# Values of an attention projected as rows ahead of it, its running products taken less one, and one copy per output

## The chip, the cores and the metric

The kernel runs on one NeuronCore of a Trainium2 chip. The metric is device time in microseconds (us) of one execution. The core's engines run side by side, each through its own row of instructions in a fixed order: TensorE (PE in the profile; PEld is its weight load) multiplies matrices, VectorE (DVE) and ScalarE (ACT) work element by element, GpSimd (POOL) does some elementwise work and starts transfers, SyncE (SP) starts most transfers. An engine waits at an instruction until what it needs is there, and everything behind it in its row waits too.

## The reference

One decoder layer on 1024 tokens of width 1024: a SwiGLU half layer, a mixer of attention and a state-space model (SSD) side by side, a cross-attention to 256 memory rows, and a second SwiGLU half layer, with RMS norms around each. What the change touches is the mixer's attention with 16 heads of 64 values, on the projections `q`, `k`, `v` of the same normalized tokens:

```python
o_att = stick_breaking_attention(heads(q), heads(k), heads(v))
...
z = jnp.einsum('bhtd,bhsd->bhts', qb, kb) * scale
causal = s_idx[None, :] < t_idx[:, None]
log_1mb = jnp.where(causal, jax.nn.log_sigmoid(-z), 0.0)
suffix = lax.cumsum(log_1mb, axis=3, reverse=True) - log_1mb
a = jnp.exp(jnp.where(causal, jax.nn.log_sigmoid(z) + suffix, -jnp.inf))
outs.append(jnp.einsum('bhts,bhsd->bhtd', a, vb.astype(jnp.float32)))
```

With beta = sigmoid(z), a[t,s] is beta[t,s] times the product of 1 − beta[t,j] over s < j < t. The product c[t,s] of 1 − beta[t,j] over s <= j < t runs backwards along s, and a[t,s] = c[t,s+1] − c[t,s], so the output for token t is a sum of running products c[t,s] times differences of value rows, v[s−1] − v[s], plus the value row v[t] of the token itself.

## The kernel before

**Number format.** Matrix products keep 32 bits by splitting each operand in a high and a low part (`split`, L265: ScalarE casts the high part, VectorE subtracts it from the source for the low one), so one product is three matmuls: high-high, high-low and low-high. `xh`/`xl` are the tokens (features on partitions, two halves of 512 tokens), `whi`/`wlo` a weight tile.

**Staging of the mixer.** The SSD comes first (`ssd`), with the projection of the memory keys woven in at its end (`keys`, evictions on L1491, stores `kv<-Bt`), then the attention (`attention`), then the output projection. Weights come through a stream (`wstream`) that loads one tile ahead, either raw and split on arrival or already split into DRAM earlier (`prepare`, `prepare_all`).

**Attention.** Eight pairs of heads, p = 0 to 7. `inproj(p)` projects `q`, `k` and `v` of the pair, each as two halves (`proj`, 24 matmuls of 512 columns into one of three PSUM banks `mm`), that is 144 matmuls. Queries and keys are evicted, split and sent to other partitions by SyncE (`rows`). For values, a half is evicted with the norm's factor (L1642), the row v[t] is stored to the output array `mix_d` in DRAM (`steps`), the differences `dv` of neighbours are formed on VectorE (L1650 to L1654), transposed on TensorE (`vtr`, four transposes of 128x128 a half) and split into the pair's value tiles V, one for each head.

`units(p)` goes through the two heads (a = 0, 1) and four chunks (c = 0 to 3) of 256 queries. `scores` makes, for each of a chunk's two blocks of 128 queries, one or two score tiles in a PSUM bank `z` (two matmuls each, at most 512 keys wide), the sigmoid of −z on ScalarE (L1746) into `nb`, and the running product on VectorE (a scan, L1750, 128 to 1024 wide), where `begin` (the identity for the diagonal block) restarts the product. Then `values` does the chunk before it: groups of three or four transposes of `nb` into a PSUM bank (`tr`, two banks, and `ms`, one, in turn), a split of each into `ath` (ScalarE, L266) and `atl` (VectorE, L268), and, three groups later (`drain(3)`), four matmuls of 256 columns with V into the chunk's output. `finish` takes the output out of PSUM: ScalarE copies the two halves (products with the high and the low part of V) to 64 partitions (L1763, L1764), VectorE adds them (L1765), and POOL adds the sum to `mix_d` by an accumulating transfer (L1767).

**The order.** TensorE's instructions stand in the order in which the program issues them. For p = 0 to 6 `merge` (L157) advances `units(p)` and `inproj(p + 1)` in turns, in proportion to two planned totals, so that projection matmuls stand between score and value work; pair 7 has other work at its side (`beside`, with the splits of `before`). Rows on the other engines are set by a scheduler after priorities: `urgent` raises that of what it holds. Work put in `later` is issued when a running sum of TensorE's cost passes a given point.

```python
self.run_all(inproj(0))
...
for p in range(7):
    self.merge(units(p), 24000, inproj(p + 1), 32500)
self.merge(tail(), 26000, beside(), 21000 + 5200 * MIXED)
```

## Time and profile before

| | |
|---|---|
| median of 3 runs | 2637.03 us (2636.95 to 2639.56) |
| the profiled execution's own time | 2636.52 us |
| its span, first to last instruction | 2634.7 us |
| mean clock granted to TensorE | 0.994 of full speed |

The profile comes from one execution. A row of a group of instructions names line, engine, operation, the tiles written and read, shapes and count, then the busy time in us, the mean ns of one, and behind the second bar the idle time of the engine just before them with what ended it. A row of the timeline gives start and duration in us, and in brackets the idle time before it. A row of a window gives its bounds and length, then busy us (and instructions) of PE, PEld, DVE, ACT and POOL, the clock granted to TensorE, the share of the transfer engines and GB/s. The durations of matmuls overlap their successors: the pace is read from their starts. A row of transfers gives count, size and the median time from issue to landing. The attention stands between about 1026 and 1590 us of the span; pair p = 2 ends near 1238 us, and a pair's period is about 61 us.

### The profile page before, as it was taken

How to read it: one execution, taken by the hardware profiler on the slowest of the kernel's cores; microseconds unless marked ns; L12 is line 12 of the kernel's file. 1: busy time of each engine (PE TensorE's matmuls, PEld its weight loads, DVE VectorE, ACT ScalarE, POOL GpSimd, SP SyncE). 2: the span in 40 equal slices, each digit the busy share in tenths (PEclk: the TensorE clock that was granted, in tenths of full speed). 3: DMA queues.
4: the chain of work that ended last, by engine and by line, in shares of the span. 5: the costliest groups of instructions: out<-in, count | busy, mean ns of one | idle time of the engine just before them, and what ended most of it. 6: DMA issues, size and time to landing. Idle time of an engine off the chain costs nothing. (4 is left out here: it accounts for less than half of the span.)

```text
span 2634.7 us, 36858 instructions
## 1 busy us (share of the span) xinstructions
PE 2587.8 (98%) x12850; PEld 2155.5 (82%) x12850; DVE 1981.6 (75%) x3044; ACT 1292.3 (49%) x2300; POOL 599.4 (23%) x713
## 2 busy tenths in 40 slices
PE   9899999999999999999999999999999999999999
PEld 7688888778777778888888897888878788888887
DVE  6778887778779775777777777767556888777777
ACT  7434444545356563555555555345544433333553
POOL 2555553110100000111111110101011555452000
PEclk9999999999999999999999999999999999999999
DMA  6558888875655226655555556547558453326554
GB/s 221 170 183 286 278 272 292 279 246 182 240 184 177 81 73 196 173 149 148 141 147 132 170 153 229 192 149 249 197 185 295 140 176 116 100 97 227 188 171 152
DMA packets 212970, 489.82 MB, mean 186 GB/s; under 512 B 26544, under 2 KB 35120, under 8 KB 212784
## 3 DMA queue, kind: packets, MB, share of 16 engines
q1 hardware_dynamic: 163472, 371.58, 42.8%
q0 software_dynamic: 25984, 73.42, 9.2%
q10 hardware_dynamic: 23328, 42.48, 4.3%
q8 instruction: 101, 1.65, 0.3%
q14 instruction: 85, 0.70, 0.1%
HBM read 327.46 MB, written 138.94 MB: 177 GB/s over the span
## 5 line engine op out<-in xcount | busy, mean ns | idle before, releaser
L139 PE MATMUL mm<-xh,whi 128*128 128x512 f32 x1320 | 522.6, 405 | 7.4 <-ACT xh L273 3.0
L139 PE MATMUL mm<-xl,whi 128*128 128x512 f32 (+1 forms) x1252 | 488.1, 390 | 4.7 <-DVE xl L268 4.4
L139 PE MATMUL mm<-xh,wlo 128*128 128x512 f32 x1272 | 489.0, 392 | 0.0
L139 PEld LDWEIGHTS mm<-xh,whi 128*128 128x128 f32 x1320 | 249.1, 189 | 50.3 <-ACT xh L266 3.9
L139 PEld LDWEIGHTS mm<-xh,wlo 128*128 128x128 f32 x1272 | 238.9, 188 | 52.0 <-DVE wlo L268 0.2
L139 PEld LDWEIGHTS mm<-xl,whi 128*128 128x128 f32 x1252 | 236.6, 189 | 39.3 <-DVE xl L268 6.3
L1750 DVE TENSOR_TENSOR_SCAN nb<-nb,begin 128x128 f32<-128x128 f32 (+7 forms) x128 | 171.5, 1352 | 52.4 <-ACT nb L1746 51.9
L1746 ACT ACTIVATE nb<-z,scale 128x128 f32<-128x128 f32 (+2 forms) x192 | 107.7, 580 | 77.8 <-PE z L139 77.5
L268 DVE TENSOR_TENSOR wlo<-wraw,whi 128x1024 fp32r<-128x1024 f32 x70 | 85.4, 1221 | 54.8 <-ACT whi L266 51.4
L266 ACT CAST whi<-wraw 128x1024 fp32r<-128x1024 f32 (+1 forms) x87 | 83.8, 964 | 79.2 <-PE mm L139 55.2
L1767 POOL DMA_DIRECT2D mix<-sq x64 | 52.9, 826 | 229.1 <-DVE sq L1765 131.0
L658 ACT ACTIVATE ft<-ft 128x512 f32<-128x512 f32 x88 | 55.5, 632 | 98.1 <-DVE ft L657 96.1
L139 PE MATMUL dn<-xh,wlo 128*128 128x512 f32 x296 | 101.3, 390 | 0.0
L741 POOL TENSOR_TENSOR wc<-wraw,raw 128x512 f32<-128x512 f32 x56 | 80.3, 1433 | 64.7 <-DVE whi L268 17.8
L741 POOL TENSOR_TENSOR wc<-raw,wraw 128x512 f32<-128x512 f32 x55 | 81.1, 1474 | 51.0 <-DVE blk L268 21.6
L268 DVE TENSOR_TENSOR atl<-tr,ath 128x512 fp32r<-128x512 f32 (+1 forms) x108 | 67.9, 632 | 29.9 <-ACT ath L266 29.5
L826 POOL TENSOR_TENSOR ft<-ft,e 128x512 f32<-128x512 f32 x37 | 59.7, 1613 | 121.1 <-DVE e L825 45.1
L139 PE MATMUL mm<-ath,v 128*128 128x256 f32 x320 | 86.1, 292 | 0.1
L266 ACT CAST ath<-tr 128x512 fp32r<-128x512 f32 (+1 forms) x108 | 58.8, 546 | 55.5 <-PE tr L142 50.9
L139 PE MATMUL dn<-xh,blk 128*128 128x512 f32 x264 | 85.2, 389 | 0.0
L266 ACT CAST wlo<-wc 128x512 fp32r<-128x512 f32 x79 | 49.1, 621 | 71.0 <-PE dn L139 26.1
L139 PE MATMUL mm<-atl,v 128*128 128x256 f32 x320 | 83.1, 282 | 0.7 <-DVE atl L268 0.7
(566 smaller groups left out, 6799.7 us busy)
## 6 DMA issues: line engine op xcount, KB each, us to landing
whi<-dwhi SPq DMA_DIRECT2D x82, 512.0 KB, 3.6
wlo<-dwlo SPq DMA_DIRECT2D x82, 512.0 KB, 4.7
wraw<-in_w_gu SPq DMA_DIRECT2D x43, 512.0 KB, 4.1
raw<-in_w_gu SPq DMA_DIRECT2D x37, 512.0 KB, 4.2
dwhi<-bh SPq DMA_DIRECT2D x66, 256.0 KB, 4.1
dwlo<-bl SPq DMA_DIRECT2D x66, 256.0 KB, 4.3
wraw<-xs SPq DMA_DIRECT2D x56, 256.0 KB, 3.1
xs<-ft ACTq DMA_DIRECT2D x54, 256.0 KB, 3.3
```

What stands on the lines that cost most here:

```text
L139: self._pe(self.nc.tensor.matmul(out, lhsT, rhs, start=start, stop=stop, skip_group_check=self.more), cost)
L266: self.kp(self.nc.scalar.copy(hi, src))
L268: self.nc.vector.tensor_tensor(out=lo, in0=src, in1=hi.bitcast(F32), op=ALU.subtract)
L658: nc.scalar.activation(t, t, AF.Silu)
L741: nc.gpsimd.tensor_tensor(out=t, in0=a, in1=b, op=op)
L826: nc.gpsimd.tensor_tensor(out=t1, in0=t1, in1=e, op=ALU.mult)
L1746: nc.scalar.activation(nb[:, s0:s1], z[:, 0:n], AF.Sigmoid, scale=sc[:, i : i + 1])
L1750: nc.vector.tensor_tensor_scan(out=nb[:, 0:Wd][:, ::-1], data0=nb[:, 0:Wd][:, ::-1], data1=begin[:, S - Wd : S][:, ::-1], initial=0.0, op0 ...
L1767: nc.gpsimd.dma_start(out=self.mix_d[p][a * 64 : a * 64 + 64, csl], in_=o, accum_op=ALU.add)
```

## The change

**Values as rows.** A new `value_rows` projects the values of all 16 heads ahead of `inproj(0)`. Tokens are the stationary operand (128 at a time) and the weights the moving one (512 columns, four head pairs), so that the result has tokens on partitions and needs no transpose. It goes in two halves of the value width, each with four weight tiles (`w_v`, raw, split on arrival), eight blocks of 128 tokens in eight PSUM banks at once (three `mm`, two `z`, two `tr`, one `ms`) and six matmuls for each tile and block: 384 matmuls. ScalarE evicts a block with the norm's factor; POOL's transfers move the block by one row to make v[s−1] (127 rows, and one from the block before); VectorE subtracts; the difference is split and stored to DRAM by POOL, for each of 16 stores as 1024 pieces of 512 bytes. `inproj(p)` fetches the pair's two value tiles (`fetch`, 512 KB each, on SyncE's queue) and projects queries and keys alone: 96 matmuls.

**Running products less one.** `begin` is now a triangle, and evicting the transposes subtracts one: ScalarE by an activation with a bias of −1, VectorE by an operation with a scalar (x − 1 − high part). With c − 1 in place of c the sum needs no value row v[t], so none is stored.

**Output.** `finish` makes one copy of 128x256 on ScalarE, and POOL writes the upper half and accumulates the lower half one output later (`added`). The last output keeps the addition.

**Beside it.** The memory keys' evictions (L1491) are marked urgent. The weight stream of the SSD goes on into the attention, so the value weights are loaded and split at the SSD's end. Sixteen halves of output weights are prepared in the SSD in place of fourteen halves of query, key and value weights there, and none is prepared in the attention. The totals of `merge` are the same as before.

```diff
@@ ssd
-                    nc.vector.tensor_tensor(out=t, in0=ps, in1=rm, op=ALU.mult)
+                    with self.urgent():
+                        nc.vector.tensor_tensor(out=t, in0=ps, in1=rm, op=ALU.mult)
...
-            W = self.wstream(
+            W = self.W = self.wstream(
                 [self.wsrc("ssd", i % 6 if i < 12 else i) for i in range(26)] + [self.wsrc("kv", i) for i in range(8)]
+                + [ap["w_v"][i] for i in range(8)] + [self.wsrc("qk", i) for i in range(16)]
             )
...
-                        [("qkv", i) for i in range(QKV, 24)], *self.prep_pool(wsp),
-                        [self.clock + 9000 + 8000 * i for i in range(2 * (24 - QKV))],
+                        [("out", i) for i in range(8, 16)], *self.prep_pool(wsp),
+                        [self.clock + 9000 + 8000 * i for i in range(16)],
@@ attention
-            self.prepare([("out", i) for i in range(8, 16)], *self.prep_pool(wsp), [self.clock + 30000 + 20000 * i for i in range(16)])
...
-            nc.vector.tensor_copy(begin[:, S - P : S], self.ident)
+            nc.vector.tensor_copy(begin[:, S - P : S], self.tri)
...
-            W = self.wstream([self.wsrc("qkv", i) for i in range(24)])
+            W = self.W
+            V_d = self.value_rows(sp, pp, W)
@@ inproj
-                V = [self.t(sp, [P, 8, P], F32R, "v", bufs=3) for _ in range(2)]
+                V = [self.t(sp, [P, 8, P], F32R, "v", bufs=4) for _ in range(2)]
...
+                def fetch(a):
+                    nc.sync.dma_start(out=V[a].bitcast(F32), in_=V_d[p // 4][:, 2 * (p % 4) + a].bitcast(F32))
...
+                if p:
+                    fetch(0)
                 qevac((yield from self.proj(wq, 0)), h0)
-                qevac((yield from self.proj(wq, 1)), h1)
-                wk = next(W)
-                kevac(evac((yield from self.proj(wk, 0)), 0), h0)
-                wv = next(W)
-                tv = []
-                t0 = evac((yield from self.proj(wv, 0)), 0)
-                tv.append(steps(0, t0, None))
-                v1 = self.proj(wv, 1)
...
+                if p < 7:
+                    qevac((yield from self.proj(wq, 1)), h1)
+                    wk = next(W)
+                    kevac(evac((yield from self.proj(wk, 0)), 0), h0)
+                    if not p:
+                        fetch(0)
+                    fetch(1)
...
                 last = self.proj(wk, 1)
                 for n in range(6):
                     next(last)
                     if p == 7:
                         before(3 + n)
                     yield
-                    if n in (2, 5):
-                        vtr(n // 3, tv[n // 3])
-                        yield
                 kevac(evac((yield from last), 1), h1)
@@ finish
-                    r = slice(64 * n, 64 * n + 64)
-                    tl, o = both[r, 0:256], both[r, 256:512]
-                    nc.scalar.copy(tl, av[64:128, :])
-                    nc.scalar.copy(o, av[0:64, :])
-                    nc.vector.tensor_tensor(out=o, in0=o, in1=tl, op=ALU.add)
-                    csl = slice(c * 256, (c + 1) * 256)
-                    nc.gpsimd.dma_start(out=self.mix_d[p][a * 64 : a * 64 + 64, csl], in_=o, accum_op=ALU.add)
+                    o = both[:, 256 * n : 256 * n + 256]
+                    out = self.mix_d[p][a * 64 : a * 64 + 64, c * 256 : (c + 1) * 256]
...
+                    nc.scalar.copy(o, av)
+                    nc.gpsimd.dma_start(out=out, in_=o[0:64, :])
+                    added()
+                    lows.append((out, o[64:128, :]))
+
+            lows = []
+
+            def added():
+
+                if lows:
+                    out, x = lows.pop()
+                    nc.gpsimd.dma_start(out=out, in_=x, accum_op=ALU.add)
@@ transpose
-                    self.split(ath[:, n0:4, :], atl[:, n0:4, :], tr[:, n0:4, :])
+                    hi, lo, x = ath[:, n0:4, :], atl[:, n0:4, :], tr[:, n0:4, :]
+                    nc.scalar.activation(hi, x, AF.Identity, bias=self.minus)
+                    nc.vector.scalar_tensor_tensor(
+                        out=lo, in0=x, scalar=-1.0, in1=hi.bitcast(F32), op0=ALU.add, op1=ALU.subtract
+                    )
@@ new
+    def value_rows(self, sp, pp, W):
...
+        def shift(tb):
+            x, y = rows[tb]
+            self.kp(nc.gpsimd.dma_start(out=y[1:P], in_=x[0 : P - 1]))
...
+        def differ(n, tb):
+            x, y = rows[tb]
+            self.kp(nc.vector.tensor_tensor(out=y, in0=y, in1=x, op=ALU.subtract))
+            o = rows[n, tb] = self.t(sp, [P, KT, P], F32R, "v", bufs=4)
+            y = y.rearrange("p (h d) -> p h d", h=8)
+            self.split(o[:, :, 0:64], o[:, :, 64:128], y)
+
+        def store(n, tb):
+            self.kp(nc.gpsimd.dma_start(out=V_d[n][:, :, tb].bitcast(F32), in_=rows.pop((n, tb)).bitcast(F32)))
+
+        for n in range(2):
...
+            for q in range(4):
+                wh, wl = next(W)
+                for tb in range(8):
+                    hh, c = tb // 4, slice(tb % 4 * P, tb % 4 * P + P)
+                    for j in range(2):
+                        k = 2 * q + j
+                        b = [w[:, 4 * j : 4 * j + 4, :].rearrange("p a b -> p (a b)") for w in (wh, wl)]
+                        self.mm3(ps[tb], [(self.XH[hh][k][:, c], self.XL[hh][k][:, c], *b)], k == 0, k == 7)
+                    if q < 3:
+                        continue
...
+                    with self.urgent():
+                        nc.scalar.activation(x[:, 0], ps[tb], AF.Copy, scale=self.C[hh][:, tb % 4 : tb % 4 + 1])
+                    at(600, shift, tb)
+                    at(6000, differ, n, tb)
+                    at(8500, store, n, tb)
```

The order of instructions shows where this moves work. Tile numbers stand behind the names; the scan is called SCALAR_TENSOR_TENSOR with `begin` here. On TensorE, at the scores of the second head's third chunk (blocks of 640 and 768 keys) in a middle pair, before:

```order
L139 MATMUL z_12954<-k_12105,q_12103 128x256
L139 MATMUL z_12954<-k_12105,wraw_9838 128x256
L139 MATMUL z_12960<-k_12105,q_12103 128x384
L139 MATMUL z_12960<-k_12105,wraw_9838 128x384
L139 MATMUL mm_12907<-xh_1441_6488,whi_12422 128x512
L139 MATMUL mm_12907<-xl_1493_6699,whi_12422 128x512
L139 MATMUL mm_12907<-xh_1441_6488,wlo_12423 128x512
L139 MATMUL z_12970<-k_12105,q_12103 128x384
L139 MATMUL z_12970<-k_12105,wraw_9838 128x384
L139 MATMUL mm_12907<-xh_1442_6489,whi_12422 128x512
L139 MATMUL mm_12907<-xl_1498_6723,whi_12422 128x512
L139 MATMUL mm_12907<-xh_1442_6489,wlo_12423 128x512
```

The same place now:

```order
L138 MATMUL z_12712<-k_11678,q_11676 128x384
L138 MATMUL z_12712<-k_11678,ql_10397 128x384
L138 MATMUL z_12716<-k_11678,q_11676 128x256
L138 MATMUL z_12716<-k_11678,ql_10397 128x256
L138 MATMUL z_12722<-k_11678,q_11676 128x384
L138 MATMUL z_12722<-k_11678,ql_10397 128x384
L138 MATMUL z_12726<-k_11678,q_11676 128x384
L138 MATMUL z_12726<-k_11678,ql_10397 128x384
L141 MATMUL ms_12731<-ident_112,nb_12685 128x128
L141 MATMUL ms_12731<-ident_112,nb_12691 128x128
L141 MATMUL ms_12731<-ident_112,nb_12685 128x128
L141 MATMUL ms_12731<-ident_112,nb_12691 128x128
```

The triples of projection matmuls (`mm` from `xh`, `xl`) are gone from this place: the four half projections of the next pair end about 20 rows above it, and the next projection matmul comes with the next pair's first scores. On VectorE, from the scan of 384 keys of the second head to its scan of 896 or 1024, before:

```order
L1750 SCALAR_TENSOR_TENSOR nb_12911<-nb_12911,begin_9832 128x384
L1750 SCALAR_TENSOR_TENSOR nb_12920<-nb_12920,begin_9832 128x512
L268 TENSOR_TENSOR atl_12928<-tr_12926,ath_12927 128x384
L1750 SCALAR_TENSOR_TENSOR nb_12946<-nb_12946,begin_9832 128x640
L1750 SCALAR_TENSOR_TENSOR nb_12959<-nb_12959,begin_9832 128x768
L216 TENSOR_TENSOR bl_12967<-braw_12505,bh_12966 128x512
L268 TENSOR_TENSOR atl_12981<-tr_12979,ath_12980 128x512
L268 TENSOR_TENSOR xl_2199_9847<-mm_12907,xl_2198_9846 128x512
L268 TENSOR_TENSOR atl_12999<-ms_12997,ath_12998 128x384
L1765 TENSOR_TENSOR sq_2191_9831<-sq_2191_9831 64x256
L1750 SCALAR_TENSOR_TENSOR nb_13036<-nb_13036,begin_9832 128x896
L1750 SCALAR_TENSOR_TENSOR nb_13049<-nb_13049,begin_9832 128x1024
```

And now:

```order
L1733 SCALAR_TENSOR_TENSOR nb_12685<-nb_12685,begin_9823 128x384
L1733 SCALAR_TENSOR_TENSOR nb_12691<-nb_12691,begin_9823 128x512
L1787 SCALAR_TENSOR_TENSOR atl_12699<-tr_12697,ath_12698 128x384
L1733 SCALAR_TENSOR_TENSOR nb_12711<-nb_12711,begin_9823 128x640
L1733 SCALAR_TENSOR_TENSOR nb_12721<-nb_12721,begin_9823 128x768
L1787 SCALAR_TENSOR_TENSOR atl_12733<-ms_12731,ath_12732 128x512
L1787 SCALAR_TENSOR_TENSOR atl_12746<-tr_12744,ath_12745 128x384
L1733 SCALAR_TENSOR_TENSOR nb_12761<-nb_12761,begin_9823 128x896
L1733 SCALAR_TENSOR_TENSOR nb_12771<-nb_12771,begin_9823 128x1024
L1787 SCALAR_TENSOR_TENSOR atl_12783<-tr_12781,ath_12782 128x512
L1787 SCALAR_TENSOR_TENSOR atl_12800<-ms_12798,ath_12799 128x512
```

The prepared weights (`bl`), the projection's split (`xl`) and the output's addition (`sq`) are gone from between the scans; scans and evictions of transposes follow one another. On VectorE around the last memory keys, ahead of the attention, before:

```order
L268 TENSOR_TENSOR Bt_9682<-sq_2160_9716,Bt_9682 128x256
L1491 TENSOR_TENSOR sq_2165_9752<-mm_9727,Ct_9206 128x256
L268 TENSOR_TENSOR dg_9890<-mm_9862,sq_2212_9889 128x512
L268 TENSOR_TENSOR Bt_9754<-sq_2165_9752,Bt_9754 128x256
L1491 TENSOR_TENSOR sq_2168_9782<-mm_9757,Ct_9206 128x256
```

And now:

```order
L267 TENSOR_TENSOR wlo_9896<-wraw_9893,whi_9895 128x1024
L267 TENSOR_TENSOR Bt_9683<-sq_2160_9717,Bt_9683 128x256
L1491 TENSOR_TENSOR sq_2165_9753<-mm_9728,Ct_9207 128x256
L339 RECIPROCAL cy_2172_9794<-cy_2172_9794 128x8
L267 TENSOR_TENSOR Bt_9755<-sq_2165_9753,Bt_9755 128x256
L1491 TENSOR_TENSOR sq_2171_9789<-mm_9764,Ct_9207 128x256
```

A split of value weights (`wlo` from `wraw`) has come in ahead of the last keys, and the first split of query rows (`dg`) is gone from between them; the last key's eviction still stands behind the split `Bt` of the key before it.

76 lines of the change are left out of this document (44 added, 32 removed).

## Prediction

> **What bounds the kernel now.** First the page's busy shares, then its matmul rate in windows of one head pair each.
>
> ```profile
> span 2634.7 us, 36858 instructions
> PE 2587.8 (98%) x12850; PEld 2155.5 (82%) x12850; DVE 1981.6 (75%) x3044; ACT 1292.3 (49%) x2300; POOL 599.4 (23%) x713
> ```
>
> ```profile
> 1177.20:1238.30 61.10, 60.45 (x355) 52.43 (x354) 45.11 (x64) 34.20 (x72) 9.21 (x24) 1.00 0.55 151
> ```
>
> TensorE is busy 98% of the span, and in a head pair's period of 61.1 us for all but 0.65 us (61.10 − 60.45), at full clock. VectorE is busy 45.11 of the 61.1 us there, so a saving in TensorE's work saves time as long as VectorE keeps up. Where it doesn't already, the groups of TensorE's instructions between 1060 and 1483 us (the end of pair 0 and pairs 1 to 6) tell, the waits standing last; the timeline shows one such wait.
>
> ```profile
> L142 PE MATMUL tr<-ident,nb 128*128 128x128 f32 x329 | 50.8, 273 | 2.2 <-DVE atl L268 1.4 <-DVE v L268 0.8
> L142 PE MATMUL ms<-ident,nb 128*128 128x128 f32 x160 | 24.9, 273 | 1.7 <-DVE v L268 1.6
> L142 PE MATMUL tr<-ident,dv 128*128 128x128 f32 x36 | 5.4, 272 | 0.0
> L142 PE MATMUL ms<-ident,dv 128*128 128x128 f32 x20 | 3.0, 272 | 0.0
> ```
>
> ```profile
> 1175.29 0.28 PE L139 MATMUL mm<-atl,v 128*128 128x256 f32 x1
> 1176.36 0.52 PE L142 MATMUL ms<-ident,nb 128*128 128x128 f32 x3 [0.80 <-DVE v L268]
> ```
>
> TensorE's only waits are at the pair ends, for VectorE's evictions of transposes: 2.2 + 1.7 = 3.9 us over six pair ends. Counted in starts, the one shown is 1176.36 − 1175.29 less 0.12 for the matmul itself, 0.95 us against the profile's 0.80; with 0.15 more each, all six are 4.8.
>
> **The change part by part.** It is costed by TensorE's pace, from starts in the timeline near the end of a pair:
>
> ```profile
> 1169.10 0.34 PE L139 MATMUL z<-k,q 128*128 128x384 f32 x1
> ...
> 1169.44 0.39 PE L139 MATMUL mm<-xh,whi 128*128 128x512 f32 x1
> ...
> 1170.14 0.39 PE L139 MATMUL z<-k,q 128*128 128x512 f32 x1
> ...
> 1170.60 0.40 PE L139 MATMUL mm<-xh,whi 128*128 128x512 f32 x1
> ...
> 1171.76 0.60 PE L142 MATMUL ms<-ident,dv 128*128 128x128 f32 x4
> 1172.19 0.60 PE L142 MATMUL tr<-ident,nb 128*128 128x128 f32 x4
> ```
>
> A score pair takes 0.34 us at 384 columns and 0.46 at 512; four transposes 0.43; a 512-column matmul half of 0.46, 0.23, and a 256-column one 0.12.
>
> *Values moved.* 8 pairs x 48 matmuls become one block of 384 ahead of inproj(0), 384 x 0.23 = 88 us at either place: 0.
>
> *Transposes of the value differences.* 64 of them go, in 16 groups of 0.43: **−7.0**. (The rows above show 56, those in that stretch.)
>
> *Old waits at pair ends.* Their releasers, the splits of transposed values (L268, v), go, or their place moves: five of the six are gone, 4.8 x 5/6: **−4.0**; the sixth, before pair 7, belongs to the p = 6 term.
>
> *The fill.* The merge still advances scores and values by 24000 against 32500 for the projections, but inproj(p + 1) is now 4 half projections (96 matmuls) and not 6 (144). By the order, it is used up before the scores of the second head's second chunk. From there to the end of the pair TensorE has scores, transposes and products alone, where before a triple of projection matmuls stood between nearly all of them. VectorE's work for that stretch is unchanged in kind: it is now a chain against less TensorE work. Its durations, and ScalarE's last:
>
> ```profile
> L268 DVE TENSOR_TENSOR atl<-tr,ath 128x512 fp32r<-128x512 f32 x31 | 21.2, 684 | 12.3 <-ACT ath L266 12.1
> L1750 DVE TENSOR_TENSOR_SCAN nb<-nb,begin 128x1024 f32<-128x1024 f32 x8 | 18.2, 2276 | 1.2 <-ACT nb L1746 1.2
> L1750 DVE TENSOR_TENSOR_SCAN nb<-nb,begin 128x896 f32<-128x896 f32 x8 | 16.2, 2024 | 6.2 <-ACT nb L1746 6.2
> L1750 DVE TENSOR_TENSOR_SCAN nb<-nb,begin 128x768 f32<-128x768 f32 x8 | 14.0, 1753 | 0.1
> L1765 DVE TENSOR_TENSOR sq<-sq 64x256 f32<-64x256 f32 x32 | 13.4, 419 | 6.1 <-ACT sq L1764 5.5
> L268 DVE TENSOR_TENSOR atl<-tr,ath 128x384 fp32r<-128x384 f32 x23 | 12.6, 546 | 1.3 <-ACT ath L266 1.3
> L1750 DVE TENSOR_TENSOR_SCAN nb<-nb,begin 128x640 f32<-128x640 f32 x8 | 11.9, 1492 | 12.0 <-ACT nb L1746 12.0
> ...
> L1750 DVE TENSOR_TENSOR_SCAN nb<-nb,begin 128x512 f32<-128x512 f32 x8 | 9.8, 1225 | 2.5 <-ACT nb L1746 2.5
> L1750 DVE TENSOR_TENSOR_SCAN nb<-nb,begin 128x384 f32<-128x384 f32 x8 | 7.7, 958 | 7.2 <-ACT nb L1746 7.2
> ```
>
> ```profile
> L1746 ACT ACTIVATE nb<-z,scale 128x384 f32<-128x384 f32 x40 | 23.2, 579 | 26.0 <-PE z L139 26.0
> ```
>
> ```profile
> L275 DVE SCALAR_TENSOR_TENSOR xl<-S,params,xh 128x512 fp32r<-128x512 f32 x16 | 11.2, 746 | 1.2 <-ACT xh L273 1.2
> ```
>
> Scans 384 to 1024: 0.96 + 1.23 + 1.49 + 1.75 + 2.02 + 2.28 = 9.73. The eviction of four transposes is now x − 1 less the high half, a form with a scalar, as L275: 0.75 for 0.68, and by the same step 0.61 for 0.55. Between the first of these scans and the transposes that wait, the order has four: 0.61 + 0.75 + 0.61 + 0.75 = 2.72. Neighbours on VectorE overlap by about 0.08 (an estimate), 9 x 0.08 = 0.7 off. Ahead of the first scan lie its score pair and sigmoid, 0.34 + 0.58, and some 0.2 of handing on. The chain: 9.73 + 2.72 − 0.7 + 1.1 = 12.8 us.
>
> TensorE's work over the same stretch: five score pairs of 384, four of 512, one of 256 and the next pair's 128 and 256: 1.70 + 1.84 + 0.24 x 2 + 0.17 = 4.2; three groups of four transposes and three of three, 3 x 0.43 + 3 x 0.33 = 2.3; six products of 4 x 0.12, 2.9; two triples of projections, 1.4. Sum 10.8. The wait is 12.8 − 10.8 = 2.0 us, mostly in front of the next pair's first transposes, whose bank is freed behind the scan of 1024. For p = 0 to 5: 6 x 2.0 = **+12.0**. It can't be under zero; if VectorE is still at work on earlier rows when the stretch begins (the last projection's eviction and split, 2 x 0.68), it is 2.8 each. Bounds 0 and +17.
>
> At the end of p = 6, VectorE's order has more ahead of the scan of 1024: four splits of 0.75 for pair 7's side work, the last key's eviction and split of 0.68 each, and two evictions of transposes that stand behind that scan in other pairs (0.75 + 0.61). 12.8 + 3.0 + 1.4 + 1.4 − 0.6 (overlaps) = 18.0, so the wait is 18.0 − 10.8 = 7.2 at most; some of the splits may run in idle time. I take **+6**, bounds +2 and +8.
>
> *The block's start.* All eight banks are taken at once; its third block waits for the bank of the last memory key (L1491). VectorE and the stores there before:
>
> ```profile
> 1027.78 0.42 DVE L1491 TENSOR_TENSOR sq<-mm,Ct 128x256 f32<-128x256 f32 x1
> 1032.86 0.69 DVE L268 TENSOR_TENSOR dg<-mm,sq 128x512 fp32r<-128x512 f32 x1 [4.66 <-ACT sq L266]
> ```
>
> ```profile
> kv<-Bt SPq DMA_DIRECT2D x3, 512.0 KB, 4.0
> ```
>
> The last key's eviction stands behind a split that waits for a store of 4.0 us to land, about 1027.7 + 4.0 = 1031.7, while the block reaches its third bank near 1029: +2.7. Marking the evictions urgent moves one of them by a sum (0.7), at a wait of TensorE near 1015: −0.7. **+2**, bounds −0.7 and +3.5. The three splits of value weights that join VectorE's row there (1.22 us each) stand in front of evictions that are awaited only at that same bank.
>
> *The output.* One copy of 128x256 for two of 64x256, no VectorE addition (8 x 0.42 us a pair off VectorE), and two transfers for one on POOL's queue. The addition isn't in the chain above: 0. The copy after next waits for a transfer to land:
>
> ```profile
> mix<-sq POOLq DMA_DIRECT2D x53, 64.0 KB, 2.9
> ```
>
> Write and accumulation one after the other are 2 x 2.9 = 5.8 us, in which ScalarE may stand, at two outputs that come soon after each other; VectorE's lag of 2 us covers part. 0, bound +1.5 a pair. Preparation of 16 halves of output weights moves out of attention into the part before it, in place of 14 others, on engines that TensorE doesn't wait for there: 0.
>
> *The clock.* What a wait of 2 us does to TensorE's granted clock:
>
> ```profile
> 1017.47 0.36 PE L139 MATMUL mm<-xs,whi 128*128 128x256 f32 x1 [1.93 <-DVE sq L1491]
> ```
>
> ```profile
> 1018.50:1021.80 3.30, 3.30 (x18) 3.30 (x17) 0.18 (x1) 0.41 (x1) 0.00 (x0) 0.50 0.65 262
> 487.30:490.70 3.40, 3.17 (x13) 2.28 (x14) 3.40 (x7) 2.71 (x6) 0.00 (x0) 1.00 0.65 214
> ```
>
> ```profile
> 487.27 0.96 PE L139 MATMUL dn<-hl,dx 128*128 128x512 f32 x3 [2.74 <-ACT F L1064]
> ```
>
> A wait of 1.93 us was followed by half clock, one of 2.74 by full clock, so the length alone doesn't decide; 3.4 us at half clock cost 1.7 us. Of the seven new waits of 2 us and more I let three cost that, since the rows go one to one: **+5**, bounds 0 and +12. [...]
>
> **The sum.** −7.0 − 4.0 + 12.0 + 6 + 2 + 5 = +14. The profiled execution took 2636.5 us (span 2634.7 and 1.8 around it), half a us under the median of 2637.03. 2636.5 + 14 = 2650.5, against the median 2651.
>
> **The rivals.**
> - *VectorE isn't late.* It loses 8 x 0.42 us of additions, the value evictions, differences and splits in each pair, so it may start the stretch with scans in hand. If the wait per pair falls under 0.5 us, the clock holds, and the end of pair 6 costs 2: −7 − 4 + 3 + 2 + 0 = −6, 2631. Deciding point: 1.0 us a pair, where gain and cost balance at about 2637 to 2639. For it speaks 45 busy of 61 us; against it, that this is a mean, and the scans of the second head stand last in the pair in the row of VectorE. 0.12; within 0.2% (under 5.3 us, about what a measurement can tell from no change), at 1 us each, 0.14.
> - *The value rows come late.* Each of 16 stores cuts its 512 KB into 1024 pieces of 512 bytes on POOL's queue, and the differences on VectorE stand in front of the queries' evictions of inproj(0).
>
> ```profile
> q0 software_dynamic: 25984, 73.42, 9.2%
> ```
>
>   A packet there takes 0.092 x 16 x 2634.7 / 25984 = 0.15 us of one engine, larger ones than these; 64 to an engine are up to 9.6 us a store, 77 for eight, while the half block after them lasts 44. If the second half's shifts queue behind them, VectorE stands for some 20 us with three banks of 24 matmuls, 5.5 us each, as cover: +5 to +15 on top, 2656 to 2666. 0.16. [...]
> - *Every wait halves the clock, and ScalarE's wait for the accumulation adds 1 us a pair.* 7 x 1.7 = 12 for 5, and +7: 2665. 0.10.
>
> **How the numbers follow.** The forecast, 2643 to 2658: 0.48. Late rows 0.16, clock and ScalarE 0.10: slower 0.74 in all. Same 0.14, faster 0.12. The range goes from 2636, which leaves out the rival on the other side and a little of "same", to 2666, which leaves out the late rows' upper end.
>
> **What would show it.** The period of a pair falls from 61.1 to about 52 us (61.1 less 48 x 0.23, less 0.9 of transposes, less 0.8 of waits, plus 2 and some clock). The groups of TensorE's transposes show waits of 10 us and more for VectorE's evictions or scans in pairs 0 to 5, in place of 3.9, and none for value splits; granted clock of 0.50 stands behind some. The value block lasts 88 us with a wait of 2 to 3 near its start. Wrong would be: waits under 0.5 us at pair ends (the first rival), waits of the projections in inproj(0) for VectorE (the second), or waits for ScalarE's copies.

## The result, and the profile after

The changed kernel takes 2663.6 us (median of 4 runs, 2661.2 to 2665.7) against 2637.0 for the kernel before on the same chip: a ratio of 1.0099, 95% interval 1.0082 to 1.0117, slower by 26.6 us in the medians. The profiled executions differ by 24.7 us (span 2659.4 for 2634.7), and all sums below are made against that.

The page of the changed kernel and, from the windows, one middle pair of heads (p = 3):

```profile
span 2659.4 us, 36677 instructions
PE 2589.6 (97%) x12786; PEld 2148.0 (81%) x12786; DVE 1939.3 (73%) x2925; ACT 1287.7 (48%) x2229; POOL 661.7 (25%) x819
```

```profile
1297.04:1347.42 50.38, 49.18 (x298) 42.39 (x297) 36.23 (x43) 29.59 (x56) 13.87 (x33) 1.00 0.53 136
```

TensorE isn't busy for less: the time has gone into its waits. What it waited for between 980 and 1640 us (us in total, times, the longest; of the lines, L138 holds the matmuls, L141 the transposes, L1729 the sigmoid, L1733 the scan, L1786 and L1787 the evictions of transposes, L1491 that of the memory keys):

```profile
PE z L138 <- DMA k<-dg: 12.7, 1, 12.7
PE z L138 <- ACT nb L1729: 8.7, 14, 2.3
PE mm L138 <- DVE sq L1491: 5.5, 2, 4.3
PE tr L141 <- DVE nb L1733: 2.5, 2, 2.3
PE ms L138 <- DVE atl L1787: 1.7, 1, 1.7
```

The longest row is one wait: the first scores of pair 0 wait for transfers of key rows (`k<-dg`, their low parts). In the timeline of TensorE, three of its four largest waits there (the fourth, of 2.28 us, is shown with pair 6 below):

```profile
1028.78 0.50 PE L138 MATMUL mm<-whi,xh 128*128 128x512 f32 x1 [4.28 <-DVE sq L1491]
...
1149.48 0.44 PE L138 MATMUL z<-k,q 128*128 128x128 f32 x1 [12.68 <-DMA k<-dg]
...
1508.81 0.55 PE L141 MATMUL tr<-ident,nb 128*128 128x128 f32 x3 [2.32 <-DVE nb L1733]
```

Cut at the same instructions, read from their starts in both traces:

| stretch | before | after | difference |
|---|---|---|---|
| up to the last norm of the SSD (`ms<-small,yacc`) | 1024.8 | 1019.6 | −5.2 |
| from there to pair 0's first scores | 35.4 | 129.9 | +94.4 |
| pair 0 | 55.9 | 47.5 | −8.4 |
| pairs 1 to 5 | 305.4 | 251.2 | −54.2 |
| pair 6 | 61.7 | 56.2 | −5.4 |
| pair 7 and up to the last norm (`ms<-small,asum`) | 117.7 | 123.0 | +5.3 |
| the rest | 1033.9 | 1032.0 | −1.9 |

The moved projections are 48 matmuls a pair, 11.0 us at 0.2285 from one start to the next. Seven pairs' worth moves up: 76.8 us out of the third to fifth row into the second. What is left is +17.6 before pair 0, +2.6 in pair 0, +0.6 in pairs 1 to 5 together, +5.6 in pair 6, +5.3 in pair 7, and −7.1 outside. Of the 5.2 us gained ahead, 2.9 are there already near 770 us, where the instructions of both kernels are the same: windows at half clock lie elsewhere in the two executions, before at 550.9 to 557.7 and 670.3 to 673.8 us, now at 486.8 to 493.7.

Half clock behind the two longest waits, and while TensorE stood, in windows of the changed kernel:

```profile
1029.60:1032.90 3.30, 3.30 (x9) 2.65 (x8) 0.03 (x1) 0.00 (x0) 0.41 (x1) 0.50 0.39 159
1139.00:1149.40 10.40, 0.00 (x0) 0.00 (x0) 0.93 (x2) 1.90 (x2) 0.00 (x0) 0.50 0.92 250
1149.50:1155.80 6.30, 6.30 (x17) 5.14 (x18) 2.07 (x3) 1.42 (x3) 0.00 (x0) 0.50 1.04 291
```

The first and the third cost 1.7 and 3.2 us of work at half speed; the second cost nothing, since TensorE waited. So the 17.6 and 2.6 us around pair 0's start are 12.7 + 3.2 for the key rows, and 4.3 + 1.7 for the last memory key's bank, 21.9 in all, less 1.7 for the four groups of transposes of value differences (0.43 each) that are gone from these two stretches.

**Why the key rows came late.** ScalarE in that place, then the transfers issued from 1100 to 1150 us (count, size, median us to landing):

```profile
1135.18 0.62 ACT L265 CAST sq<-ev 128x512 fp32r<-128x512 f32 x1 [2.93 <-DMA q<-sq]
1144.53 0.62 ACT L265 CAST xl<-ev 128x512 fp32r<-128x512 f32 x1 [8.73 <-DMA q<-xl]
```

```profile
v<-v POOLq DMA_DIRECT2D x8, 512.0 KB, 8.3
...
q<-sq SPq DMA_DIRECT2D x4, 128.0 KB, 7.7
q<-xl SPq DMA_DIRECT2D x4, 128.0 KB, 7.6
```

The split of the first key half waits until the first query half's rows have left the same buffer, the second likewise. Those rows take 7.7 us to land, where they took 4.9 in the kernel before at the same place and 3.5 in its pair 2. Eight stores of value rows, 512 KB each, are under way; that these are the reason is tested below (e5). SyncE's own issue of them stretches too:

```profile
1131.96 3.07 SPq L1631 DMA_DIRECT2D q<-xl  x2
1135.12 1.87 SPq L1631 DMA_DIRECT2D wraw<-xl  x1
```

so that the key rows, behind them in SyncE's row, are issued at 1142.8 us only. The first key half is split by 1138.6 already, and SyncE's row has no gap of more than 0.3 us from 1121.1 to 1142.8: what ended last is that row, not the buffer. TensorE had finished all 96 projections at 1136.8.

### The profile page after: what moved, and what is told of

The parts are those of the page before. It is cut to its first block, busy times and chain, and to the rows that moved or that the text cites. A ratio compares the mean times of both kernels' runs of the same rounds, so it can differ in the third digit from the quotient of the medians.

```text
span 2659.4 us, 36677 instructions
## 1 busy us (share of the span) xinstructions
PE 2589.6 (97%) x12786; PEld 2148.0 (81%) x12786; DVE 1939.3 (73%) x2925; ACT 1287.7 (48%) x2229; POOL 661.7 (25%) x819
## 4 chain that ended last, share of the span: by engine, by line
PE 82%; DVE 7%; issue 4%; DMA 4%; ACT 2%; POOL 1%; SPq 0%; DVEq 0%; ACTq 0%; POOLq 0%
PE mm L138 42%; PE dn L138 31%; PE z L138 2%; DVE nb L1733 2%; PE ms L138 1%; PE tr L141 1%; PE y L138 1%; PE ms L141 1%; PE seg L138 1%; PE tr L138 1%; DVE atl L1787 1%; PE st L138 0%; DVE hl L267 0%; SPq L1631 0%; DMA oraw<-mix 0%
## 5 line engine op out<-in xcount | busy, mean ns | idle before, releaser
L138 PE MATMUL mm<-xh,whi 128*128 128x512 f32 x1192 | 470.0, 404 | 3.6 <-ACT xh L265 2.7
L138 PE MATMUL mm<-xl,whi 128*128 128x512 f32 (+1 forms) x1124 | 438.6, 390 | 4.7 <-DVE xl L267 4.1
L138 PE MATMUL mm<-xh,wlo 128*128 128x512 f32 x1144 | 439.0, 392 | 0.0
L138 PEld LDWEIGHTS mm<-xh,whi 128*128 128x128 f32 x1192 | 225.3, 189 | 45.5 <-ACT xh L265 3.9
L138 PEld LDWEIGHTS mm<-xh,wlo 128*128 128x128 f32 x1144 | 215.2, 188 | 46.6 <-DVE wlo L267 0.4
L138 PEld LDWEIGHTS mm<-xl,whi 128*128 128x128 f32 x1124 | 212.6, 189 | 39.1 <-DVE xl L267 6.2
L1733 DVE TENSOR_TENSOR_SCAN nb<-nb,begin 128x128 f32<-128x128 f32 (+7 forms) x128 | 169.9, 1349 | 57.0 <-ACT nb L1729 56.8
L267 DVE TENSOR_TENSOR wlo<-wraw,whi 128x1024 fp32r<-128x1024 f32 x78 | 95.3, 1222 | 89.1 <-ACT whi L265 88.7
L1729 ACT ACTIVATE nb<-z,scale 128x128 f32<-128x128 f32 (+2 forms) x192 | 105.4, 582 | 68.4 <-PE z L138 68.0
L138 PE MATMUL dn<-xh,wlo 128*128 128x512 f32 x296 | 101.2, 390 | 0.0
L1786 ACT ACTIVATE ath<-tr,small 128x512 fp32r<-128x512 f32 (+1 forms) x106 | 68.3, 646 | 50.9 <-PE tr L141 49.1
L1787 DVE SCALAR_TENSOR_TENSOR atl<-tr,ath 128x512 fp32r<-128x512 f32 (+1 forms) x106 | 65.7, 625 | 36.0 <-ACT ath L1786 35.5
L138 PE MATMUL z<-k,q 128*128 128x128 f32 (+2 forms) x192 | 68.0, 358 | 21.4 <-DMA k<-dg 12.7
L138 PE MATMUL mm<-ath,v 128*128 128x256 f32 x320 | 88.6, 299 | 0.0
L138 PE MATMUL dn<-xh,blk 128*128 128x512 f32 x264 | 85.2, 389 | 0.0
L138 PE MATMUL mm<-atl,v 128*128 128x256 f32 x320 | 83.2, 282 | 0.5 <-DVE atl L1787 0.5
```

The source lines that it names most:

```text
L138: self._pe(self.nc.tensor.matmul(out, lhsT, rhs, start=start, stop=stop, skip_group_check=self.more), cost)
L267: self.nc.vector.tensor_tensor(out=lo, in0=src, in1=hi.bitcast(F32), op=ALU.subtract)
L1729: nc.scalar.activation(nb[:, s0:s1], z[:, 0:n], AF.Sigmoid, scale=sc[:, i : i + 1])
L1733: nc.vector.tensor_tensor_scan(out=nb[:, 0:Wd][:, ::-1], data0=nb[:, 0:Wd][:, ::-1], data1=begin[:, S - Wd : S][:, ::-1], initial=0.0, op0 ...
L1786: nc.scalar.activation(hi, x, AF.Identity, bias=self.minus)
L1787: nc.vector.scalar_tensor_tensor(out=lo, in0=x, scalar=-1.0, in1=hi.bitcast(F32), op0=ALU.add, op1=ALU.subtract)
```

## The experiments

The runs were made at different times, each beside runs of the kernel before (medians of 2636.99 to 2639.61), so the ratio to it, or the difference of the two medians, is what compares. Of the first three experiments the intervals overlap with the changed kernel's; what they did is read from their traces. Each edit is made to the changed kernel. One more, e5, leaves out work, was executed once, and has no interval.

| run | ratio to the kernel before | interval | us above the kernel before |
|---|---|---|---|
| the change | 1.0099 | 1.0082 to 1.0117 | 26.6 |
| e1_k_second | 1.0085 | 1.0069 to 1.0100 | 24.4 |
| e2_whole_rows | 1.0076 | 1.0061 to 1.0091 | 21.2 |
| e3_mm_banks_last | 1.0069 | 1.0054 to 1.0084 | 20.1 |
| e4_fill_even | 1.0044 | 1.0028 to 1.0061 | 12.3 |
| e6_two_copies | 1.0108 | 1.0091 to 1.0126 | 29.8 |
| e7_values_after_pair0 | 1.0066 | 1.0051 to 1.0081 | 18.4 |
| e8_first_even_banks | 1.0032 | 1.0019 to 1.0045 | 8.5 |
| e9_three_together | 1.0019 | 1.0007 to 1.0030 | 5.5 |
| e10_and_fetch_late | 1.0022 | 1.0012 to 1.0032 | 5.6 |
| e11_cover_for_pair0 | 1.0010 | 1.0001 to 1.0018 | 2.9 |
| e12_cover_and_block_later | 1.0028 | 1.0018 to 1.0038 | 8.0 |

### The key rows of pair 0

**e1: keys in the second place.**

```diff
-                    qevac((yield from self.proj(wq, 1)), h1)
+                    if p:
+                        qevac((yield from self.proj(wq, 1)), h1)
                     wk = next(W)
                     kevac(evac((yield from self.proj(wk, 0)), 0), h0)
                     if not p:
+                        qevac((yield from self.proj(wq, 1)), h1)
                         fetch(0)
```

> Pair 0 alone projects in the order q, k, q, k of the halves (it was q, q, k, k), so that the first half of the keys is evicted 24 matmuls (5.5 us) earlier, into the split buffer that no transfer holds; the two fetches stand behind the second query half. Theory A (the first keys wait for the split buffer that the first queries' transfers still hold, and have only 24 matmuls as cover): the wait of 12.7 us at pair 0's first scores falls to about 4, and half of the 17 us at half clock goes, 2663.6 - 8.7 - 1.5 = about 2653. Theory B (all transfers there are slow because the value stores fill the engines, whatever the order): the wait stays above 9, 2660 or more.

Median 2663.3. TensorE's waits:

```profile
PE z L138 <- DMA k<-xl: 4.8, 1, 4.8
PE z L138 <- issue: 2.7, 1, 2.7
```

The one wait of 12.7 us has become two, 2.7 at the first scores (for which the profile names no releaser) and 4.8 when the second half of the keys is needed. From the SSD's end to pair 1 the trace is 3.7 us shorter, less than half of what theory A gave. The order was one cause, but the run can't tell how: the edit gives the keys another buffer and also moves their rows ahead of the second query half's in SyncE's row. The slow landing stays, now on the other half.

**e2: the value rows stored whole.**

```diff
-        V_d = [self.tc.dram_tile([P, 8, KT, P], F32R, name=self.nm("v")) for _ in range(2)]
+        V_d = [self.tc.dram_tile([P, KT, 8, P], F32R, name=self.nm("v")) for _ in range(2)]
...
-out=V_d[n][:, :, tb].bitcast(F32)
+out=V_d[n][:, tb].bitcast(F32)
```

> The value rows lie in DRAM as they are stored: a store is 128 pieces of 4 KB in place of 1024 of 512 bytes, and a pair's fetch takes the small pieces in its place. Theory B: the stores land in about 4 us in place of 7.0, the query and key rows in 3 in place of 7.7, and the wait of 12.7 us falls under 5, about 2653. Theory A alone: the stores aren't what the rows wait for, the wait stays at 10 or more, 2660 to 2665. If the fetch in small pieces holds up SP's queue in every pair, waits for k or v come in at pair starts and it is slower than 2664.

Median 2660.0. The stores landed in 6.0 us where it was 7.0, and the wait was 11.0 us for 12.7. In e6, which doesn't touch this, it was 11.0 as well, so the pieces' size did next to nothing: theory B, as it put it by pieces, falls. The bytes are the same. The median, by the table 5.4 us better than the change, does not speak for the pieces either: the intervals overlap, and the traced execution took 2664.2 us.

**e5: no stores of the second half.**

```diff
-                    at(8500, store, n, tb)
+                    if not n:
+                        at(8500, store, n, tb)
```

> Leaves out the eight stores of the second half's value rows (pairs 4 to 7 then fetch those of pairs 0 to 3, so heads 8 to 15 get other heads' values); all else as changed. In the changed kernel the transfer engines were 97 to 99% busy from 1113 to 1137 us, with 4 MB of these stores, and finer or coarser pieces made no difference. Theory (the bytes of the stores make the query and key rows land in 7.7 us): without them the rows land in 4 us or less and the wait of 12.7 us at pair 0's first scores falls to 3 or less with no half clock, about 2648. Rival (SyncE's slow issue, 1.2 to 1.9 us for one row transfer there, has another reason, or the split buffers alone): the wait stays above 7.

One execution, 2651.0 us. The transfers from 1100 to 1150 us, and TensorE's wait:

```profile
q<-sq SPq DMA_DIRECT2D x5, 128.0 KB, 2.9
...
k<-dg SPq DMA_DIRECT2D x2, 128.0 KB, 3.1
```

```profile
PE z L138 <- DMA k<-dg: 0.3, 1, 0.3
```

The wait is gone with the half clock behind it. As far as one execution tells, that is 12.1 us above the kernel before (2638.95 beside it) where the change is 26.6. The stores are what the key rows waited for, by their bytes rather than their pieces (e2): from 1113 to 1137 us the transfer engines are busy 0.94 of the time in the changed kernel's trace (not the 97 to 99% of the expectation) and 0.86 here, and one row's issue on SyncE takes 0.5 to 1.0 us again. With the rows landing in 2.9 us the buffers no longer hold anything up either, so e1's cause is a consequence of this one.

### The last key's bank, and the fill

**e3: the mm banks last.** In the list of eight banks `z`, `z`, `tr`, `tr`, `ms` come first and the three `mm` behind them.

> The block's eight banks are taken in another order: z, z, tr, tr, ms first and the three mm banks, which the memory keys still hold, for the last three token blocks. If the 4.3 us near 1025 are the wait for the last key's eviction, they go, with the 3.4 us at half clock behind them: 2663.6 - 4.3 - 1.7 = about 2657.5. Rival: the block then waits at its eviction end or the queries' first half waits for an mm bank, and nothing is gained: 2663.

Median 2659.0, by the table 6.5 us less than the change, about the 6.0 expected. The wait of 4.3 us is gone and with it the window at half clock near 1030; of the row for L1491 the wait near 1015 is left:

```profile
PE mm L138 <- DVE sq L1491: 1.3, 1, 1.3
```

**e4: the fill spread over the pair.**

```diff
-                self.merge(units(p), 24000, inproj(p + 1), 32500)
+                self.merge(units(p), 24000, inproj(p + 1), 20700)
```

> The merge gets 20700 in place of 32500 for the four half projections, so that they last to the end of each pair. Where the fill ran out, the trace of the changed kernel shows waits of scores for sigmoids (1.5 us a pair in starts, pairs 1 to 5), and 2.3 + 0.4 + 0.7 + 2.3 us at the end of pair 6. Theory (the fill's end makes them): they go in pairs 0 to 5 (6 x 1.5 = 9 us) and 3 of pair 6's 5.7, about 2652. Rival (VectorE's and ScalarE's work is what the pair now takes): the waits spread over the pair and the period stays at 50.4 us, 2660 or more.

Median 2651.2, by the table 14.3 us less than the change, the most of any single edit that leaves no work out. A middle pair, and the waits for sigmoids that are left (8.7 in the changed kernel):

```profile
1345.00:1393.91 48.91, 48.64 (x298) 42.40 (x297) 36.31 (x43) 30.07 (x57) 13.86 (x32) 1.00 0.58 141
```

```profile
PE z L138 <- ACT nb L1729: 4.0, 8, 1.3
```

The pair takes 48.9 us for 50.4, with the same 36 us of VectorE, so the fill's end, not the pair's work, made the waits. In the traces pairs 0 to 5 are 8.0 us shorter, against the 9 expected. Pair 6 and what follows up to the last norm are 5.6 shorter: the waits for scans are gone there, those of scores for sigmoids are down to 1.3 and 1.1, and no half clock follows.

### The output

**e6: two copies and the addition, as before the change.**

```diff
-                    nc.scalar.copy(o, av)
-                    nc.gpsimd.dma_start(out=out, in_=o[0:64, :])
+                    nc.scalar.copy(tl, av[64:128, :])
+                    nc.scalar.copy(o, av[0:64, :])
+                    nc.vector.tensor_tensor(out=o, in0=o, in1=tl, op=ALU.add)
+                    nc.gpsimd.dma_start(out=out, in_=o)
...
```

> Undoes the output part alone: two copies of 64x256 on ScalarE, VectorE's addition, one plain transfer of POOL for each output, no accumulation. VectorE gets 8 x 0.42 us a pair, ScalarE 8 x 0.37. If the output part gave anything it is in the stretch without fill, where two outputs fall: scores wait longer by up to 0.37 an output there, +3 to +5 over seven pairs, 2667 to 2669. Rival (the wait for the accumulation to land costs ScalarE as much): 2663, no difference.

Median 2668.7, by the table 3.2 us worse than the change, though the intervals overlap. In the trace the period of pair 3 is longer by 0.6 us, as the expectation had it:

```profile
1294.97:1345.95 50.98, 49.37 (x298) 42.39 (x297) 39.23 (x51) 32.81 (x65) 7.05 (x24) 1.00 0.46 124
```

With the change, ScalarE's copies wait for the accumulation to land (10.5 us over pairs 1 to 5, six times). In those pairs TensorE has no more than a wait of 0.3 us near them, for an eviction, and e6, without accumulation, has the same one. In pair 6 it is otherwise (below).

### Other orders, and the edits together

**e7: the value block behind pair 0's queries and keys.** `run_all(inproj(0))` stands ahead of `value_rows`, pair 0's fetches behind it; the raw tiles and three of the token blocks use other buffers.

> The queries and keys of pair 0 are projected first, the value block behind them (its raw tiles and blocks in other buffers; the weight stream in that order), and pair 0's fetches behind the block. The rows of queries and keys then have 88 us to land, and the last memory key's bank isn't awaited, since the projections take banks one at a time. Theory: 12.7 us and their 3.3 of half clock go, and 4.3 with 1.7 of half clock; pair 0's scans now share VectorE and ScalarE with the second half's differences and splits (16 of 0.69 on VectorE), which costs 2 to 6 in pair 0. 2663.6 - 22 + 4 = about 2646. Rival (the second half's value rows then hold up pair 0 by as much): 2655 or more.

Median 2657.4, against the 2646 expected. The waits for key rows and for the last key's bank are gone, as expected, but pair 0 takes 56.5 us for 47.5: its scores and transposes wait for ScalarE and VectorE, in whose rows the second half's differences and splits now stand. The rival comes nearer.

**e8: e7, e3 and e4 together.**

> The order of the values behind pair 0's queries and keys, the mm banks last in the block, and the fill spread over each pair (20700). The savings add if they are at different places: 2646 - 12 = about 2634, level with the kernel before or a little under. Rival (the even fill takes from pair 0 what the order gave): 2640 or more.

Median 2647.5, the rival's side, not the 2634 of the expectation. Pair 0 and pair 1 in windows:

```profile
1133.75:1195.02 61.27, 49.24 (x255) 40.78 (x253) 40.10 (x49) 31.50 (x57) 19.58 (x37) 0.92 0.69 203
1195.02:1243.93 48.91, 48.65 (x297) 42.42 (x296) 35.41 (x41) 29.53 (x55) 12.60 (x30) 1.00 0.55 139
```

In pair 0 TensorE has 42 matmuls fewer than in pair 1 (fewer transposes and products, which follow one chunk behind the scores) and takes 12.4 us longer all the same: it waits 12.0 us, and three windows of 3.4 us are at half clock.

**e9: e1, e3 and e4 together.**

> The fill spread (20700), the mm banks last, and pair 0's halves in the order q, k, q, k, together, with the value block ahead of pair 0 as changed. If the three savings lie at three places they add: 2663.6 - 12.4 - 4.6 - 3.7 (the last from the traces, from the SSD's end to pair 1) = about 2643. The first scores still wait for k rows, 3 to 5 us twice. Rival: the even fill gives pair 0 more to do while the second half's stores run, 2648.

Median 2644.1: by the table 21.1 us less than the change, where the three alone give 2.2 + 6.5 + 14.3 = 23.0, so within the intervals (some 3 us each way) the savings add. Two waits are left where the key rows are needed, 4.5 us (no releaser named) and 5.0.

**e10: e9 with pair 0's fetches behind its keys.**

> As the run before, and pair 0's two fetches (1 MB) stand behind the second half of its keys on SyncE's queue instead of ahead of it. If the second wait (4.8 us for k rows, with half clock) is made by the 1 MB ahead of them, it goes: 2643 - 5 = about 2638. Rival: the values come late instead, pair 0's first products wait by 2 to 5 us, and the sum is level with the run before.

Median 2644.1. The expected 5 us didn't come: the second wait isn't shorter but longer, 7.4 us. The megabyte of the fetches wasn't what it waited for.

**e11: e9, with 17 triples of pair 1's projections ahead of pair 0's scores.**

```diff
-                self.merge(units(p), 24000, inproj(p + 1), 32500)
+                fill = inproj(p + 1)
+                for _ in range(0 if p else 17):
+                    next(fill)
+                self.merge(units(p), 24000, fill, 20700 if p else 9700)
```

> The three edits together (fill spread, mm banks last, pair 0 in the order q, k, q, k), and 17 of the 32 triples of projections for pair 1 stand ahead of pair 0's first scores (11.7 us), the other 15 being spread over pair 0. If the waits for pair 0's key rows (4.5 and 5.0 us, and 6.8 us of half clock after them) are a lack of other work for TensorE while the transfers are held up by the value stores, they go, and pair 0 with half its fill pays about 2 us: 2644.1 - 9.5 - 3 + 2 = about 2633.5, faster than the kernel before by 0.2%. Rival (pair 0 with half the fill is bound by VectorE and ScalarE): 2640 or more.

Median 2642.5, ratio 1.0010, the nearest to the kernel before, but in the rival's range and not the 2633.5 expected. The wait of TensorE is now one place further, in the projections themselves:

```profile
PE mm L138 <- DVE xl L267: 6.5, 1, 6.5
```

The third `mm` bank is held by a half whose split waits for a buffer that rows under way still hold (ScalarE's longest wait for `k<-xl` is 6.5 us there). Cover by more projections fills banks, not time.

**e12: e8 with the same 17 triples.**

> The same 17 triples ahead of pair 0's scores, with the value block behind pair 0's queries and keys. Here pair 0 waited for sigmoids and evictions (1.85 + 2.3 + 1.4 + 2.9 + 3.1 us, and three windows at half clock) while the second half's differences and splits ran on VectorE and ScalarE; the 11.7 us cover most of that: 2647.5 - 9 = about 2638. Rival: VectorE's row keeps the same work and pair 0 ends no sooner, 2645.

Median 2647.6, as e8: the rival's time. The trace has another reason for it than VectorE's row. ScalarE stands in front of splits of value differences whose buffer a store (`v<-v`) still holds, and TensorE's two longest waits, for sigmoids, end right behind. ScalarE, then TensorE:

```profile
1147.77 0.62 ACT L268 CAST v<-nb 128x512 fp32r<-128x512 f32 x1 [7.23 <-DMA v<-v]
...
1156.86 0.62 ACT L268 CAST v<-nb 128x512 fp32r<-128x512 f32 x1 [3.52 <-DMA v<-v]
```

```profile
1150.61 0.44 PE L138 MATMUL z<-k,q 128*128 128x384 f32 x1 [3.42 <-ACT nb L1733]
...
1158.01 0.69 PE L138 MATMUL z<-k,q 128*128 128x384 f32 x1 [3.12 <-ACT nb L1733]
```

So behind pair 0's projections, too, it is the stores that the block's new place runs into, here by the buffers that they hold. No run takes these waits away alone.

No version is faster than the kernel before. Not tried: a store of half the bytes (the differences before their split), and a second half of the value block spread over later pairs.

## Why the prediction was right, and where it wasn't

The direction was right, and the time lies in the range (2636 to 2666), near its upper end. The forecast of 2651, +14, was half of the +26.6 measured and the time lies outside the likeliest case's own range of 2643 to 2658. That the range holds it is in part luck: the largest cost was in no term of the sum. By its steps:

- **Values moved, "0".** This is the step that failed. TensorE's work is the same at either place, but the step moved two other things: 48 matmuls of cover went from between pair 0's first keys and its scores, and 4 MB of stores came in ahead of the rows that these scores need. That cost 12.7 us and 3.2 of half clock. e5 takes both away by the stores alone, with no cover added. The rival of late value rows had the stores and the right time (2656 to 2666, given 0.16), but another path: VectorE would have been held up by the differences. VectorE did stand 21.2 us in front of a difference, but in the value block, where nothing waited for it. ScalarE did stand in front of a difference's split, ahead of that of the second query half, until a store let go of the buffer:

```profile
1129.07 0.62 ACT L265 CAST v<-k 128x512 fp32r<-128x512 f32 x1 [3.00 <-DMA v<-v]
```

  But SyncE was then still at the first query half's rows, up to 1130.5 us, and began the second's at 1132.0, so this is worth 1.5 us of the 12.7 at most; what was late were SyncE's rows.
- **Transposes, −7.0, and old waits, −4.0.** TensorE has 12786 matmuls for 12850, the 64 transposes less, 0.86 us a pair, and none of its waits is for a split of values any more: right.
- **The fill, +12.0.** The size is right: pairs 1 to 5 took 61.08 us each, 48.3 without the moved matmuls (10.97), the transposes (0.86) and the old wait (0.95), and take 50.24 now, so some 1.9 a pair for 2.0 forecast. The place in the order is right too, as e4 shows. The path is wrong, by the sign that the prediction itself set: the waits at the pair ends, for VectorE's evictions, are 0.32 to 0.34 us, under its 0.5. Most of the cost, 1.5 us in starts, is ahead of them: the scores wait for a `z` bank, which ScalarE's sigmoid frees (0.44 and 0.43 us as idle time, the two in each pair). Pair 3's end and the start of the next:

```profile
1339.80 0.44 PE L138 MATMUL z<-k,q 128*128 128x384 f32 x1 [0.44 <-ACT nb L1729]
...
1343.74 0.50 PE L138 MATMUL z<-k,q 128*128 128x512 f32 x1 [0.43 <-ACT nb L1729]
...
1349.74 0.66 PE L141 MATMUL tr<-ident,nb 128*128 128x128 f32 x4 [0.32 <-DVE atl L1787]
```

  The overlap of neighbours on VectorE that the chain took off, 0.08 us, is what the trace of before shows (a split of 0.68 us from 1167.88 us on, the next from 1168.48). The chain was priced too dear by its evictions: a group of four is 0.68 us by the form with a scalar, where 0.75 was taken,

```profile
L1787 DVE SCALAR_TENSOR_TENSOR atl<-tr,ath 128x512 fp32r<-128x512 f32 x40 | 27.0, 680 | 18.1 <-ACT ath L1786 18.1
L1786 ACT ACTIVATE ath<-tr,small 128x512 fp32r<-128x512 f32 x40 | 27.7, 694 | 23.4 <-PE tr L141 23.3 <-issue 0.2
```

  and the dearer part of x − 1 is ScalarE's, 0.69 us for the 0.59 of the plain cast. It had not been costed at all, and it is ScalarE that TensorE then waits for; no run takes this part away alone, so its share is not shown.
- **The end of pair 6, +6.** Pair 6 lost 5.6 us beside the moved matmuls; 1.7 of them are half clock, counted below, and 0.9 of transposes saved stand against them, so its waits are 4.8. The last 2.3 of its chain fall into pair 7: 7.1, inside the bounds of 2 to 8. Only these 2.3 are on the path that was forecast, a transpose waiting for VectorE's scan. The longest of the others, 2.28 us, is a wait for a sigmoid, and ScalarE in front of it stood at the side work for pair 7 and then at a copy, each time for a transfer, the second the accumulation:

```profile
1488.46 0.72 ACT L272 ACTIVATE xh<-ev,params 128x512 fp32r<-128x512 f32 x1 [1.45 <-DMA ev<-mix]
1490.87 0.37 ACT L1755 COPY sq<-mm 128x256 f32<-128x256 f32 x1 [1.69 <-DMA mix<-sq]
```

```profile
1492.86 0.44 PE L138 MATMUL z<-k,q 128*128 128x384 f32 x1 [2.28 <-ACT nb L1729]
```

  Without the accumulation (e6) that wait is still 1.67 us, with ScalarE 1.99 us in front of `ev<-mix`, so the accumulation is the smaller part.
- **The block's start, +2.** 4.3 us for the bank of the last key against 2.7 forecast, and 1.26 near 1015 for the 1.93 before (0.7 less, as forecast): 3.6. e3 confirms the cause. The half clock behind it was not in this term.
- **The output, 0.** e6 makes it a gain of 0.6 us a pair: a copy less on ScalarE counts in the stretch without fill.
- **The clock, +5.** 1.7 near 1030, 3.2 in pair 0 and 1.7 near 1494, less 1.7 that the kernel before had near 1018: 4.9, but not at the ends of pairs 0 to 5, whose waits of 0.4 us left the clock full: no window at half clock lies between 1155.9 and 1493.7 us.

In sum the fill, which was priced with care, came to what it was priced at, over another engine than the one priced, and the largest single cost was in the step that was put at nothing. Of pair 7's 5.3 us, 2.3 are the end of pair 6's chain; the rest is left open. Two sums beside the forecast don't come out: 2.0 and twice 0.68 are 3.4 a pair, not the 2.8 of the fill's upper bound, and the first rival's 2631 leaves out the 2 us of the block's start. Neither moves the forecast.

## What to carry to other kernels

A block of work that is moved without loss on the busy engine still moves its transfers and takes away the cover of whatever stood behind it: here rows of 128 KB landed in 7.7 us beside the stores and in 2.9 without those of the second half (e5), and TensorE waited 12.7 us. List for the new place which transfers are then in flight, and which short ones, with a consumer waiting, have to share the engines with them. When work is taken out of an interleaved order, set its proportions anew first (here, by e4, 14 of the 26.6 us). And a buffer that is released by a transfer's landing ties the next computation to the load on the transfer engines (here a split on ScalarE stood 8.73 us until `q<-xl` had landed; from 1135.5 to 1144.5 us the transfer engines were busy 0.91 of the time).

## What the runs showed of the hardware

- In the traces of before and of the changed kernel all windows at half clock begin on one grid of 3.413 us, with another phase in each. In the changed kernel those at 1029.56, 1138.79, 1493.77 and 1620.07 us lie 32, 104 and 37 such steps apart. There a wait of 2.28 us that lay inside one cell (1490.6 to 1492.9, cell from 1490.4 to 1493.8) was followed by half clock from 1493.8, and one of 2.32 us that a cell's border cut in two (1506.5 to 1508.8, border at 1507.4) was followed by full clock. The prediction's two rows of the kernel before fit as well: the wait of 1.93 us lies inside the cell from 1015.1 to 1018.5, that of 2.74 is cut at 486.0.
- A transfer of 128 KB that lands in 2.9 us with 2.1 MB of POOL's traffic beside it (e5) takes 7.7 with 6.3 MB in the same 50 us, and SyncE's issue of one goes from some 0.5 to as much as 1.9 us. With the same 6.3 MB in pieces of 4 KB (e2) the landing was 7.4 us, so by these runs it is the bytes of the other traffic and not its pieces.
- The shifts of 127 rows out of `nb`, issued from 1060 to 1150 us of the changed kernel, landed in a median of 4.0 us:

```profile
nb<-nb POOLq DMA_DIRECT2D x10, 254.0 KB, 4.0
```
